# Six of seven projections by seven block products instead of eight, in a pooling and mLSTM trunk on one Trainium2 core

## The chip, the core and the metric

The kernel runs on one core of a Trainium2 chip. The core has five engines with queues of their own: TensorE (PE: matmuls; PEld: the loading of their stationary operand), VectorE (DVE), ScalarE (ACT), GpSimd (POOL) and SyncE (SP, which here issues every DMA). Matmuls read SBUF and write PSUM; everything else goes between SBUF and DRAM by DMA. The metric is the time of one execution on the device in microseconds (us), lower is better.

## The reference

One layer over 4096 rows (SEQ) of 1024 channels, in float32. Cut to what matters:

```
u = rmsnorm(x, norm_w)
pool_x, pool_z, m_x, m_z, m_o = split(u @ w_in, 5)       # 1024 columns each
# pooling branch: 4 groups of 256 channels, trailing windows 2, 4, 8, 16
d = window_mean(pool_x) - pool_x
y_pool = (d @ pool_w[group]) * pool_scale * silu(pool_z)
# mLSTM branch: 4 heads of 256
xc = silu(causal_conv4(m_x))
q, k, v = blockdiag(xc, xc, m_x);  i, f = gates(q, k, v)
h = mlstm_chunkwise(q, k, v, i, f)                      # chunks of 128 rows
hn = head_norm(sigmoid(m_o) * h) * mh_norm_w
y_mlstm = (hn + m_skip * xc) * silu(m_z)
out = rmsnorm(x + concat(y_pool, y_mlstm) @ w_out, final_norm_w)
```

There are seven products of a 4096 x 1024 matrix with a 1024 x 1024 one: the five parts of w_in and the two halves of w_out.

## The kernel before

Every float32 operand of a projection is split into a high part in a 32-bit matmul format and the rest (`split`, lines 88 to 90: ACT casts, DVE subtracts). `mm3` (lines 114 to 120) then makes a product as high by high, high by low and low by high, so one tile of 128 x 128 by 128 x 512 is three matmuls. One product of 512 rows with a 1024 x 1024 matrix is 4 x 2 x 8 such tiles, or 192 matmuls.

The work is in stages. **Pooling** (lines 139 to 302): eight blocks of 512 rows. `norm_u` (154 to 203) loads x transposed, makes the norm, keeps u in SBUF and stores it in DRAM (`u_d`); the block's u is split once and used for both the folded pooling projection (`fold`, 216 to 239: the group's map is multiplied into the weights beforehand) and its gate; products of the pooling go to `yp_d`. **mLSTM** (305 to 686): half blocks of 256 rows. `project` makes m_x and the convolution, `front` and `back` do one chunk of 128 rows each in steps, and the string `ORDER` (line 32) says in which order steps of front, back, next projection and convolution are issued. h goes to `h_d`, x_c to `xc_d`. In the last two chunks `gate_ahead` (401 to 416) computes the m_z gate of the last 256 rows in place of a next projection. **Gates** (690 to 774): per block of 512 rows u is loaded again, the m_z gate (`gate`) and m_o are projected, the head norm is made, `finish` transposes h and stores `ym_d`. **Output** (774 to 819): per 256 rows y_pool and y_mlstm are loaded and split, multiplied with w_out, x is added, the last norm made.

All DMAs stand in SP's queue, in the order that the scheduler of the language gives them; each engine runs its queue in order. Tiles come from pools with a fixed number of buffers, and an instruction waits until the buffer that it writes is free: weights come through two raw buffers (`wsp`), u tiles in pools of 19 or 18.

Of the kernel before, what the change touches and what calls it, by code (L numbers as in the profile page):

```python
# [12 lines left out]
ALU = mybir.AluOpType  # L13
# [6 lines left out]
NJ = D // P  # L20
T = 512
# [6 lines left out]
# gate tiles made ahead of the head norm  # L28
GA = 4
# [4 lines left out]
GW = P + 8  # L34


@with_exitstack
def tile_hybrid(
# [7 lines left out]
    pool_scale: bass.AP,  # L46
# [10 lines left out]
    NB = S // T  # L57
    DH = D // H

    const = ctx.enter_context(tc.tile_pool(name="const", bufs=1))  # L60
    w1p = ctx.enter_context(tc.tile_pool(name="w1p", bufs=16))
    stp = ctx.enter_context(tc.tile_pool(name="stp", bufs=4))
    wsp = ctx.enter_context(tc.tile_pool(name="wsp", bufs=2))
# [4 lines left out]
    col = const.tile([P, 64], F32, name="col")  # L68
# [5 lines left out]
    msk = col[:, 56:64]  # L74
    nhalf = const.tile([P, H], F32, name="nhalf")
    nc.vector.memset(nhalf, -0.5)

    u_d = [dram.tile([NJ, P, T], F32, name=f"u_d{b}") for b in range(NB)]
    yp_d = [dram.tile([NJ, P, T], F32, name=f"yp_d{b}") for b in range(NB)]
    ym_d = [dram.tile([NJ, P, T], F32, name=f"ym_d{b}") for b in range(NB)]  # L80
    xc_d = [dram.tile([NJ, P, T], F32, name=f"xc_d{b}") for b in range(NB)]
    sz_d = dram.tile([NJ, P, TB], F32, name="sz_d")
    h_d = [dram.tile([NCH, P, D], F32, name=f"h_d{b}") for b in range(NB)]

    def st():
        return stp.tile([P, D], F32, name="st")

    def split(raw, hi, lo):
        nc.scalar.copy(out=hi, in_=raw)  # L89
        nc.vector.tensor_tensor(out=lo, in0=raw, in1=hi.bitcast(F32), op=ALU.subtract)  # L90

    def load_w(src, n, pool, tag, stage=None):
        """src as [part, tile, column] in n tiles of 1024/n columns, split."""
        hi = pool.tile([P, D], F32R, name=tag)
        lo = pool.tile([P, D], F32R, name=tag)
        for h in range(2):
            raw = stage.tile([P, D // 2], F32, name="u") if stage else wsp.tile([P, D // 2], F32, name="ws")
            if n == 1:
                nc.sync.dma_start(out=raw, in_=src[:, 0, h * T:(h + 1) * T])
            else:  # L100
                nc.sync.dma_start(out=raw.rearrange("p (k c) -> p k c", k=n // 2),
                                  in_=src[:, h * n // 2:(h + 1) * n // 2, :])
            split(raw, hi[:, h * T:(h + 1) * T], lo[:, h * T:(h + 1) * T])
        return hi, lo

    def load_in_cols(c0, pool, tag, stage=None):
        """Columns c0..c0+127 of w_in by k tile: [k part, k tile, column]."""
        return load_w(w_in[:, c0:c0 + P].rearrange("(k p) c -> p k c", p=P), NJ, pool, tag, stage)

    def load_rows(w, r0, c0, n, pool, tag):  # L110
        """Rows r0.. in n tiles of 128, 1024/n columns from c0: [row part, tile, column]."""
        return load_w(w[r0:r0 + n * P, c0:c0 + D // n].rearrange("(k p) c -> p k c", p=P), n, pool, tag)

    def mm3(ps, pairs, start=True, stop=True):
        """ps = sum over pairs of (stationary hi, lo) with (moving hi, lo), without lo by lo."""
        n = len(pairs)
        for k, (a, b) in enumerate(pairs):
            nc.tensor.matmul(ps, lhsT=a[0], rhs=b[0], start=start and k == 0, stop=False)  # L118
            nc.tensor.matmul(ps, lhsT=a[0], rhs=b[1], start=False, stop=False)  # L119
            nc.tensor.matmul(ps, lhsT=a[1], rhs=b[0], start=False, stop=stop and k == n - 1)  # L120

    def kcol(pair, k):
        return tuple(t[:, k * P:(k + 1) * P] for t in pair)

    def proj_t(ps, wpair, u):
        mm3(ps, [(kcol(wpair, k), u[k]) for k in range(NJ)])

    def proj_part(ps, wpair, u, part):
        """Half of proj_t's k tiles."""
        mm3(ps, [(kcol(wpair, k), u[k]) for k in range(4 * part, 4 * part + 4)], part == 0, part == 1)  # L130

    def load_u(b, k0, k1, pool):
        u = []
        for k in range(k0, k1):
            lo = pool.tile([P, T], F32R, name="u")
            nc.sync.dma_start(out=lo.bitcast(F32), in_=u_d[b][k])
            u.append((pool.tile([P, T], F32R, name="u"), lo))
        return u

    # ---------------------------------------------------------------- pooling mixer  # L140
    with tc.tile_pool(name="a_u", bufs=19) as up, \
            tc.tile_pool(name="a_w2", bufs=16) as w2p, \
            tc.tile_pool(name="a_work", bufs=2) as wk, \
            tc.tile_pool(name="a_one", bufs=1) as one, \
            tc.tile_pool(name="a_tp", bufs=1, space=PSUM) as tpp, \
            tc.tile_pool(name="a_acc", bufs=6, space=PSUM) as accp:
        inv0 = one.tile([P, HALO], F32, name="inv0")
        nc.gpsimd.iota(inv0, pattern=[[1, HALO]], base=1, channel_multiplier=0,
# [726 lines left out]
```

## Time and profile before

| | us |
|---|---|
| median of 3 runs (3152.22 to 3162.3) | 3160.18 |
| the profiled execution: span from first to last instruction | 3157.9 |
| last wide matmul of the pooling stage starts | 751.7 |
| first wide matmul of the gates | 1731.5 |
| last wide matmul | 3150.5 |

A line of the page on an engine gives its busy time, the share of the span and its instructions. A line on a group gives source line, engine, operation, what is written and read, shape and count, then busy time and mean length of one in ns, then the idle time of the engine before it and what ended that. A window's line gives its length and then busy time and count of each engine, the granted TensorE clock (1.00 is full), the mean busy share of the 16 DMA engines and GB/s.

### The profile page before, as it was taken

The page shows a single profiled execution, that of the slowest core. Times are in us where ns is not written, and L with a number is a line of the kernel's source. Part 1 is how long each engine was busy: PE and PEld are TensorE (multiplying, and loading weights), DVE is VectorE, ACT ScalarE, POOL GpSimd, SP SyncE. Part 2 cuts the span into 40 slices and gives each one's busy share as a digit, 9 for nine tenths or more (in the row PEclk, how much of TensorE's full clock was granted, in tenths as well). Part 3 has the DMA queues.
Part 4 walks back from the last instruction along what each step waited for, and adds up shares of the span by engine and source line. Part 5 has one row for each costly group of instructions (what it writes and reads, how often), then busy time and mean ns, then how long its engine had stood idle before and what let it go on. Part 6 is the DMA issues. An engine that isn't in the chain of part 4 may idle for free.

```text
span 3157.9 us, 44492 instructions
## 1 busy us (share of the span) xinstructions
PE 3056.9 (97%) x16872; PEld 2659.8 (84%) x16872; DVE 1642.0 (52%) x3726; ACT 1162.2 (37%) x2464; POOL 573.8 (18%) x811
## 2 busy tenths in 40 slices
PE   7999999999899999999999999999999999999999
PEld 6888888888898998998998888888888788888887
DVE  5554444544788788888887443334436422222221
ACT  4221122223677677767776222222113311111111
POOL 1010010101354445444543000000000000000000
PEclk9999999999999999999999999999999999999999
DMA  6221111222111111112133223333215523222231
GB/s 210 87 77 70 61 67 60 77 97 75 61 55 58 51 54 62 50 51 64 51 91 112 76 93 107 107 107 107 68 59 173 184 100 107 94 92 96 94 107 50
DMA packets 189607, 273.57 MB, mean 87 GB/s; under 512 B 17232, under 2 KB 111952, under 8 KB 189392
## 3 DMA queue, kind: packets, MB, share of 16 engines
q1 hardware_dynamic: 189392, 270.72, 25.5%
q8 instruction: 133, 2.18, 0.3%
q14 instruction: 82, 0.67, 0.1%
HBM read 168.96 MB, written 101.71 MB: 86 GB/s over the span
## 4 chain that ended last, share of the span: by engine, by line
PE 86%; DVE 6%; DMA 3%; ACT 3%; issue 1%; SPq 1%; POOL 0%; POOLq 0%; DVEq 0%; ACTq 0%
PE acc L118 24%; PE acc L119 24%; PE acc L120 24%; DVE xc L370 3%; PE mm L603 2%; PE mm L628 2%; PE map L482 2%; PE mm L599 1%; DMA sk<-xc_d 1%; PE map L472 1%; PE map L493 1%; DMA ws<-in_w_out_dram 1%; PE acc L236 1%; DVE c L629 1%; PE tp L726 0%
## 5 line engine op out<-in xcount | busy, mean ns | idle before, releaser
L118 PE MATMUL acc<-u,w 128*128 128x512 f32 (+1 forms) x2592 | 907.3, 351 | 3.8 <-ACT mx L617 1.7
L120 PE MATMUL acc<-u,w 128*128 128x512 f32 (+1 forms) x2592 | 897.5, 346 | 0.0
L119 PE MATMUL acc<-u,w 128*128 128x512 f32 (+1 forms) x2592 | 895.5, 346 | 0.0
L118 PE MATMUL acc<-w,u 128*128 128x512 f32 x1536 | 598.4, 390 | 3.8 <-ACT w L89 2.8
L119 PE MATMUL acc<-w,u 128*128 128x512 f32 x1536 | 598.1, 390 | 0.2 <-DVE w L90 0.2
L120 PE MATMUL acc<-w,u 128*128 128x512 f32 x1536 | 597.5, 390 | 0.0
L118 PEld LDWEIGHTS acc<-u,w 128*128 128x128 f32 x2592 | 495.2, 191 | 64.2 <-ACT u L89 4.1
L119 PEld LDWEIGHTS acc<-u,w 128*128 128x128 f32 x2592 | 495.7, 191 | 58.6 <-DVE u L90 1.1
L120 PEld LDWEIGHTS acc<-u,w 128*128 128x128 f32 x2592 | 495.5, 191 | 57.4
L118 PEld LDWEIGHTS acc<-w,u 128*128 128x128 f32 x1536 | 288.5, 188 | 65.5 <-ACT w L89 3.6
L120 PEld LDWEIGHTS acc<-w,u 128*128 128x128 f32 x1536 | 288.9, 188 | 60.4 <-DVE u L790 0.6
L119 PEld LDWEIGHTS acc<-w,u 128*128 128x128 f32 x1536 | 288.6, 188 | 60.6 <-DVE w L90 0.7
L370 DVE SCALAR_TENSOR_TENSOR xc<-mx,col,xc 128x256 f32<-128x256 f32 x384 | 220.6, 632 | 30.5 <-POOL mx L447 22.3
L804 DVE TENSOR_TENSOR st<-acc,st 128x512 f32<-128x512 f32 x64 | 44.3, 692 | 364.9 <-PE acc L120 364.9
L356 POOL TENSOR_TENSOR cs<-c,cs 128x516 fp32r<-128x516 f32 x124 | 176.4, 1423 | 232.0 <-ACT cs L355 208.2
L757 POOL TENSOR_TENSOR rs<-rs,nhalf 128x2 f32<-128x2 f32 x64 | 44.6, 697 | 660.6 <-DVE rs L756 660.6
L789 ACT CAST u<-u 128x512 fp32r<-128x512 f32 x128 | 77.6, 619 | 230.7 <-PE acc L119 187.2
L811 ACT ACTIVATE sk<-st 128x1024 bf16<-128x1024 f32 x31 | 32.8, 1058 | 311.4 <-DVE st L804 311.4
L815 POOL TENSOR_TENSOR rso<-ssq,nhalf 128x1 f32<-128x1 f32 x32 | 17.4, 543 | 701.9 <-DVE ssq L812 701.9
L749 DVE SCALAR_TENSOR_TENSOR st<-th,st 128x512 f32<-128x512 f32 x64 | 44.3, 692 | 184.8 <-ACT th L747 184.7
L747 ACT ACTIVATE th<-acc 128x512 f32<-128x512 f32 x64 | 38.3, 598 | 273.4 <-PE acc L120 272.9
L599 PE MATMUL mm<-va,st 128*128 128x258 f32 x384 | 82.1, 310 | 52.3 <-DVE st L90 39.8
(181 smaller groups left out, 4201.9 us busy)
## 6 DMA issues: line engine op xcount, KB each, us to landing
u<-u_d SPq DMA_DIRECT2D x128, 256.0 KB, 3.9
st<-in_x_t_dram SPq DMA_DIRECT2D x32, 512.0 KB, 3.5
u_d<-st SPq DMA_DIRECT2D x32, 512.0 KB, 4.2
yp_d<-sg SPq DMA_DIRECT2D x64, 256.0 KB, 2.0
xc_d<-xc SPq DMA_DIRECT2D x64, 256.0 KB, 2.4
st<-h_d SPq DMA_DIRECT2D x32, 512.0 KB, 5.2
sk<-xc_d SPq DMA_DIRECT2D x64, 256.0 KB, 3.8
ym_d<-sg SPq DMA_DIRECT2D x64, 256.0 KB, 3.1
```

The source lines that it names most:

```text
L118: nc.tensor.matmul(ps, lhsT=a[0], rhs=b[0], start=start and k == 0, stop=False)
L119: nc.tensor.matmul(ps, lhsT=a[0], rhs=b[1], start=False, stop=False)
L120: nc.tensor.matmul(ps, lhsT=a[1], rhs=b[0], start=False, stop=stop and k == n - 1)
L356: nc.gpsimd.tensor_tensor(out=t[:, 1], in0=cst[h], in1=t[:, 0].bitcast(F32), op=ALU.subtract)
L370: nc.vector.scalar_tensor_tensor(out=a[:, t], in0=m[:, t, i:i + TB], scalar=conv_w[:, jj * 4 + i:jj * 4 + i + 1], in1=a[:, t], op0=ALU.mul ...
L482: nc.tensor.matmul(ps[:, i, :], lhsT=bqk[:, q * 4 + i, :], rhs=xc[q * 4 + i][:, l0:l0 + P], start=True, stop=True)
L599: nc.tensor.matmul(nps, lhsT=wt[:, w, h, :], rhs=vh[v], start=i == 0, stop=first and i == 2)
L603: nc.tensor.matmul(nps, lhsT=qi[h][:, w, t, :], rhs=cs[:, v, t], start=False, stop=t == 1 and i == 2)
L628: nc.tensor.matmul(upd, lhsT=xw[h][:, w, t * P:(t + 1) * P], rhs=vh[v], start=i == 0, stop=i == 2)
L749: nc.vector.scalar_tensor_tensor(out=hv, in0=th, scalar=1.0, in1=hv, op0=ALU.add, op1=ALU.mult)
L757: nc.gpsimd.tensor_tensor(out=rs, in0=rs, in1=nhalf[:, 0:2], op=ALU.pow)
L789: nc.scalar.copy(out=hi, in_=raw)
```

## The change

The pooling projection and its gate, the output gate, the m_z gate and both output projections are now made in "passes", each one 1024-column product over four blocks of 1024 rows. Rows, inner dimension and columns of a block are halved, and the eight products of quarters become seven, by sums of quarters on either side and sums of results. The m_x projection of the mLSTM stretch keeps eight.

- Left operands are kept in DRAM as quarters ready to use (`us_d`, `yp_d`, `ym_d`: a11, s2, a12, s3, s1, a22, s4, a21), so the sums are made once by `put_sums` where u or y is made, on POOL (for the first block half on DVE).
- Right operands are summed as they are loaded (`load_right`: raw tiles through a pool of 8, sums on POOL, then the split). A pass keeps its seven in SBUF; the next pass's are loaded during the last of its four blocks.
- `drive` runs 14 steps per block (7 products, two halves of the inner dimension, 24 matmuls each). Left tiles are fetched from DRAM and split for every pass, up to three steps ahead.
- Results are combined in `Item.after` on DVE, partly by accumulating two products in one PSUM bank. What follows a result (pooling, gate, head norm, residual, last norm) hangs on `done` of an item.
- The order is: two pooling passes (each half of the pooling columns with half of the gate's), the first output pass (x + y_pool w_out into `r_d`), mLSTM, output gate (into `hn_d`), m_z gate (into `ym_d`), second output pass and last norm.
- `norm_next` makes the next block's u during the first pass and loads its x twice. The mLSTM's weights are loaded at the end of the first output pass; `gate_ahead` is gone, and in its place the first four of the output gate's right operands are loaded. `pool_scale` is applied by ACT after the gate's SiLU instead of in the fold.

```
+A_OF = ("a11", "s2", "a12", "s3", "s1", "a22", "s4", "a21")
+NP = 7
+B_OF = (((1, 0, 0),),
+        ((1, 1, 1), (-1, 0, 1), (1, 0, 0)),
+        ((1, 1, 0),),
+        ((1, 1, 1), (-1, 0, 1)),
+        ((1, 0, 1), (-1, 0, 0)),
+        ((1, 1, 0), (-1, 1, 1), (1, 0, 1), (-1, 0, 0)),
+        ((1, 1, 1),))
+AHEAD = 4
...
+    def load_right(hi, lo, k, terms, sources, tile):
+        acc = None
+        for sign, kh, ch in terms:
+            t = tile()
+            rows, c0 = sources[ch]
+            nc.sync.dma_start(out=t, in_=rows(k + 4 * kh)[:, c0:c0 + T])
+            if acc is not None:
+                nc.gpsimd.tensor_tensor(out=acc, in0=acc, in1=t, op=ALU.add if sign > 0 else ALU.subtract)
+            else:
+                acc = t
+        split(acc, hi[:, k], lo[:, k])
...
+        def fetch(t):
+            n, r, i, kh = steps[t]
+            hi = ring.tile([P, 2, T], F32R, name="sr")
+            lo = ring.tile([P, 2, T], F32R, name="sr")
+            raw = lo.bitcast(F32)
+            nc.sync.dma_start(out=raw, in_=passes[n].left[r][i][:, 2 * kh:2 * kh + 2, :])
+            split(raw, hi, lo)
+            got[t] = hi, lo
...
+            for v in range(t, min(t + AHEAD, len(steps))):
+                if v not in got:
+                    fetch(v)
...
+            chain = "abab" "cbc"[i]
...
+                mm3(ps, pairs, start=kh == 0 and i in (0, 1, 4), stop=kh == 1, skip=True)
+                if kh == 1:
+                    f = p.items[q].after(r, i, ps)
...
+            if r + 1 == NR:
+                nxt = passes[n + 1] if n + 1 < len(passes) else None
+                free = i - 1 if kh == 0 else (i if i == NP - 1 else -1)
+                if free >= 0 and nxt:
+                    load(nxt, free)
...
+        def after(self, r, i, ps):
+            v = self.view
+            if i == 0:
+                self.s1 = self.tile()
+                nc.scalar.copy(out=v(self.s1), in_=ps)
+            elif i == 1:
+                self.u2 = self.tile()
+                nc.vector.tensor_tensor(out=v(self.u2), in0=ps, in1=v(self.s1), op=ALU.add)
+            elif i == 2:
+                return self.done(r, 0, 0, self.first(ps))
+            elif i == 3:
+                self.u3 = self.tile()
+                nc.vector.tensor_tensor(out=v(self.u3), in0=ps, in1=v(self.s1), op=ALU.add)
+            else:
+                t, rh, ch = ((self.u3, 1, 1), (self.s1, 1, 0), (self.u2, 0, 1))[i - 4]
+                nc.vector.tensor_tensor(out=v(t), in0=ps, in1=v(t), op=ALU.add)
+                return self.done(r, rh, ch, t)
...
+    with tc.tile_pool(name="a_w2", bufs=6) as w2p, \
+            tc.tile_pool(name="a_ring", bufs=8) as ring, \
+            tc.tile_pool(name="a_ch", bufs=17) as chp, \
+            tc.tile_pool(name="a_x", bufs=8) as xp, \
...
+        def norm_next(r):
+            ss = one.tile([P, 2, T], F32, name="ss")
+            for h in range(2):
+                for k in range(NJ):
+                    t = x_tile()
+                    x_load(t, r, k, h)
...
+            for k in range(4):
+                q = {}
+                for kk in (k, k + 4):
+                    for h in range(2):
+                        t = x_tile()
+                        x_load(t, r, kk, h)
+                        scaled(t, kk, ss[:, h])
+                        name = f"a{h + 1}{kk // 4 + 1}"
+                        put_quarter(us_d[r], name, k, t, put_now)
+                        q[name] = t
+                put_sums(us_d[r], k, q["a11"], q["a12"], q["a21"], q["a22"], x_tile, nc.gpsimd, put_now)
...
+        drive([*p_mix, p_out1], ring, w2p, psp, x_tile, background, load_wm)
...
+        drive([p_o, p_z, p_out2], ring, w2p, psp, x_tile, background)
```

More of the change, by code (lines that the diff above doesn't have):

```diff
@@ L89, in split @@
+    wf_d = [dram.tile([P, D], F32, name=f"wf_d{k}") for k in range(NJ)]
+    def split(raw, hi, lo, eng=None):
         nc.scalar.copy(out=hi, in_=raw)
[L90 to L114, printed above, removed]
+        (eng or nc.vector).tensor_tensor(out=lo, in0=raw, in1=hi.bitcast(F32), op=ALU.subtract)
+    def mm3(ps, pairs, start=True, stop=True, skip=False):
@@ L116, in mm3 @@
         n = len(pairs)
         for k, (a, b) in enumerate(pairs):
[L118 to L143, printed above, removed]
+            nc.tensor.matmul(ps, lhsT=a[0], rhs=b[0], start=start and k == 0, stop=False, skip_group_check=skip)
@@ new lines, in start, with loads, squares, slot @@
+        def start():
+            ss = one.tile([P, 2, T], F32, name="ss")
+            xs = {}
+            def loads(h):
+                for k in range(NJ):
+                    xs[k, h] = chp.tile([P, HALO + T], F32, name="ch")[:, 0:T]
+                    x_load(xs[k, h], 0, k, h)
+            def squares(h):
+                for k in range(NJ):
+                    if k == 0:
+                        nc.scalar.activation(out=ss[:, h], in_=xs[k, h], func=AF.Square)
+                    else:
+                        sq = x_tile()
+                        nc.scalar.activation(out=sq, in_=xs[k, h], func=AF.Square)
+                        nc.vector.tensor_tensor(out=ss[:, h], in0=ss[:, h], in1=sq, op=ALU.add)
+            free = []
+            def slot():
+                if not free:
+                    t = w2p.tile([P, 4, T], F32, name="w2")
+                    free.extend(t[:, i] for i in range(4))
+                return free.pop(0)
+            loads(0)
+            folds = [fold(g, slot) for g in range(2)]
+            next(folds[0])
+            loads(1)
+            next(folds[1])
+            squares(0)
+            root(ss[:, 0])
+            for _ in folds[0]:
+                pass
+            for _ in folds[1]:
+                pass
+            for k in range(NJ):
+                scaled(xs[k, 0], k, ss[:, 0])
+                put_quarter(us_d[0], ("a11", "a12")[k // 4], k % 4, xs[k, 0], put_now)
+            squares(1)
+            root(ss[:, 1])
+            for k in range(4):
+                for kk in (k, k + 4):
+                    scaled(xs[kk, 1], kk, ss[:, 1])
+                    put_quarter(us_d[0], ("a21", "a22")[kk // 4], k, xs[kk, 1], put_now)
+                a21 = x_tile()
+                nc.scalar.copy(out=a21, in_=xs[k, 1])
+                put_sums(us_d[0], k, xs[k, 0], xs[k + 4, 0], a21, xs[k + 4, 1], x_tile,
+                         (nc.vector, nc.gpsimd)[k % 2], put_now)
@@ new lines, in tile_hybrid, with background @@
+        p_mix = [Pass(us_d, [(wf_rows, n * T), (in_rows, D + n * T)], [Mix(n, c) for c in range(4)], False)
+                 for n in range(2)]
+        p_out1 = Pass(yp_d, halves(out_rows(0), 0), [Sum(q) for q in range(4)], True)
+        start()
+        norms = [norm_next(r) for r in range(1, NR)]
+        folds = [fold(g, x_tile) for g in range(2, H)]
+        def background(n, r, m):
+            if n == 0 and r + 1 < NR:
+                for _ in range({0: 1, 1: 1, 2: 1, 3: 1, 6: 1, 7: 1, 8: 1, 9: 1, 10: 2}.get(m, 0)):
+                    next(norms[r])
+            if n == 0 and r in (1, 2) and m in (11, 12, 13):
+                next(folds[r - 1], None)
```

693 lines of the change are left out of this document (414 added, 279 removed).

## The prediction

> **What bounds the kernel now.** I read the page's shares and chain first, then the windows by stage, then the groups of lines with shapes kept apart, then the DMA queue and its issues.
>
> ```profile
> span 3157.9 us, 44492 instructions
> PE 3056.9 (97%) x16872; PEld 2659.8 (84%) x16872; DVE 1642.0 (52%) x3726; ACT 1162.2 (37%) x2464; POOL 573.8 (18%) x811
> PE 86%; DVE 6%; DMA 3%; ACT 3%; issue 1%; SPq 1%; POOL 0%; POOLq 0%; DVEq 0%; ACTq 0%
> core 0: us, PE busy (x) PEld busy (x) DVE busy (x) ACT busy (x) POOL busy (x), PEclk, DMA share, GB/s
> 0.00:26.00 26.00, 10.94 (x37) 8.79 (x37) 14.87 (x27) 12.54 (x20) 3.61 (x10) 1.00 0.74 224
> 26.00:752.00 726.00, 725.04 (x3196) 600.06 (x3196) 360.53 (x561) 176.54 (x301) 63.66 (x137) 1.00 0.24 83
> 752.00:765.00 13.00, 11.25 (x66) 10.84 (x66) 4.47 (x14) 5.89 (x28) 0.98 (x9) 0.68 0.75 228
> 765.00:1731.00 966.00, 898.90 (x7176) 873.65 (x7176) 769.83 (x2122) 673.60 (x1623) 443.56 (x560) 0.96 0.19 61
> 1731.00:2457.00 726.00, 720.31 (x3370) 597.06 (x3370) 312.30 (x737) 174.53 (x291) 44.63 (x64) 1.00 0.31 104
> 2457.00:3158.00 701.00, 690.52 (x3031) 569.40 (x3031) 179.98 (x269) 119.15 (x203) 17.39 (x32) 0.99 0.29 100
> ```
>
> The chain is PE for 86%, and the windows show where: in the pooling stage (26 to 752) and in the last two (1731 to 3158) PE is busy all but 1 to 11 us of 700, while DVE stands at 26 to 50%, POOL at 2 to 9% and the DMA engines at 24 to 31%. Only the mLSTM stretch is mixed (PE 93%, DVE 80%, POOL 46%). A busy PE need not be PE at its peak, so the price of a matmul is read from their starts: PE's timeline at 2700 us, first and last of 55 rows, and the groups by shape.
>
> ```profile
> 2699.61 0.39 PE L120 MATMUL acc<-w,u 128*128 128x512 f32 x1
> ...
> 2711.85 0.39 PE L120 MATMUL acc<-w,u 128*128 128x512 f32 x1
> L118 PE MATMUL acc<-w,u 128*128 128x512 f32 x1536 | 598.4, 390 | 3.8 <-ACT w L89 2.8 <-ACT u L789 1.0
> L118 PE MATMUL acc<-u,w 128*128 128x512 f32 x1472 | 574.7, 392 | 3.4 <-ACT mx L617 1.7 <-ACT u L89 1.5
> L118 PE MATMUL acc<-u,w 128*128 128x256 f32 x1120 | 332.5, 298 | 0.4 <-ACT xc L453 0.4
> 1709.09 0.28 PE L120 MATMUL acc<-u,w 128*128 128x256 f32 x1
> ...
> 1711.25 0.28 PE L120 MATMUL acc<-u,w 128*128 128x256 f32 x1
> ```
>
> 12.24 us over 54 steps is **0.2267 us** for one 128x512 matmul, though its own record lasts 0.39; the 256-column form (2.16 us over 18 steps at 1709 us) takes 0.12. Lines 118 to 120 run alike, so 3 x (1536 + 1472) = 9024 of them take 2046 us. The time is bought with matmuls.
>
> **What the change removes.** Six projections over four blocks of 1024 rows are 6 x 4 x 384 matmuls by eight block products, 6 x 4 x 336 = 8064 by seven. 8064 x 0.2267 = 1828 us; so 218 us less of the wide form, and also gone are 384 of the 256-column form at 0.12 (the gate of the last rows, half of it run ahead in the mLSTM stretch): 264 us of PE in all. One block of one pass is now 336 x 0.2267 = 76.2 us of PE, a pass 305, a step of 24 matmuls 5.4.
>
> **What it adds: sums and splits.** Nearest rows:
>
> ```profile
> L90 DVE TENSOR_TENSOR w<-ws,w 128x512 fp32r<-128x512 f32 x80 | 54.4, 688 | 48.0 <-ACT w L89 47.6
> L89 ACT CAST w<-ws 128x512 fp32r<-128x512 f32 x80 | 48.9, 620 | 78.7 <-DMA ws<-in_w_in_dram 37.8 <-DMA ws<-in_w_out_dram 30.4 <-PE acc L119 8.7
> L434 POOL TENSOR_TENSOR u<-u 128x512 fp32r<-128x512 f32 x64 | 85.3, 1335 | 105.3 <-ACT u L433 105.3
> L817 DVE SCALAR_TENSOR_TENSOR st<-st,rso,fw 128x1024 f32<-128x1024 f32 x31 | 39.8, 1285 | 22.3 <-POOL rso L815 22.3
> L753 DVE BATCH_NORM_STATS2 stats<-st 128x6 f32<-128x256 f32 x128 | 48.2, 418 | 2.1
> L754 DVE BATCH_NORM_AGGREGATE mv<-stats 128x2 f32<-128x6 f32 x128 | 19.2, 173 | 0.0
> ```
>
> DVE in one block of the output-gate pass, the fullest plain one: 14 splits of 1024 columns at 1.285 (18), 20 adds out of PSUM at 0.69 (14), 16 products with h (11), 32 statistics at 0.418 and 0.173 (19), small ones (5): 67 us beside 76 of PE. POOL in the first pass: 16 adds of sums, 14 of squares, 8 products at 1.335 and small copies, about 60. Both lie beside PE, and I cost them at nothing. In the block in which the next pass's weights are loaded, 28 splits (DVE 19) and 28 adds (POOL 37) come on top: DVE 86, POOL 76 to 80. That cover is gone there, and the excess of up to 10 us is taken to lie under the transfers, below. Each left tile is fetched three steps (16 us) ahead, and landing, cast and subtract take 3.9 + 1.1 + 1.3, so a single fetch is hidden.
>
> **What it adds: transfers.** This is the term that decides. Everything now goes through DRAM: seven left quarters per block and pass, the sums, the residual, the normalised h.
>
> ```profile
> q1 hardware_dynamic: 189392, 270.72, 25.5%
> u<-u_d SPq DMA_DIRECT2D x128, 256.0 KB, 3.9
> st<-in_x_t_dram SPq DMA_DIRECT2D x32, 512.0 KB, 3.5
> u_d<-st SPq DMA_DIRECT2D x32, 512.0 KB, 4.2
> ws<-in_w_in_dram SPq DMA_DIRECT2D x48, 256.0 KB, 3.1
> ws<-in_w_out_dram SPq DMA_DIRECT2D x32, 256.0 KB, 3.3
> w<-in_wx_t_dram SPq DMA_DIRECT2D x8, 512.0 KB, 7.9
> ```
>
> I count in tiles of 256 KB (0.262 MB). Per block: left operand 28 in each pass. First pooling pass: 32 loads of x (twice 16), 32 stores of u and its sums, 8 of the product, 100 in all for the first three blocks and 36 for the last; 9 for a folded group in two blocks. Second: 8 products, 8 reads, 16 sums, 60. First output pass 60; output gate 28 + 16 h + 16 stores = 60; gate path 28 + 16 + 16 + 28 = 88; last pass 60. The weights of a pass are 14 terms x 4 = 56 tiles, all but the mLSTM's 16 loaded in the last block of the pass before (the output gate's half in the mLSTM stretch, half in its first block). The whole is some 2290 tiles, 600 MB against 271.
>
> At what rate? The best that 20 us of this trace held, a start, and the rest:
>
> ```profile
> 2000.00:2020.00 20.00, 19.52 (x95) 15.68 (x94) 10.67 (x17) 8.72 (x15) 0.00 (x0) 1.00 0.88 310
> 20.00:50.00 30.00, 27.55 (x122) 22.54 (x121) 24.86 (x41) 17.99 (x31) 4.06 (x5) 1.00 0.86 282
> ```
>
> 310 GB/s at a share of 0.88 would be 352 at a share of 1; the start held 282 over 30 us and 224 over 26. I take **310**, 0.846 us a tile, the nearest row that is a burst of these same tile loads, and keep 352 and 224 as ends (2991 and, by 1.17 us a tile and 103 us in each other block of the gate path, 3432). The 512-byte rows of the h tiles cost nothing more: the weight columns (512-byte rows) land in 3.1 us, the output weights (2 KB rows) in 3.3. Where tiles x 0.846 is under PE's time, the transfer is hidden; where it is over, it sets the time:
> - first pass with the launch: start 16 + 32 + 18, weights 56, blocks 100 + 109 + 109, last block 36 + 56: 532 tiles, 450 us, against some 365 of PE work (305, the folds and the launch);
> - last block of the second pooling pass: 60 + 56 = 116 tiles, 98 us against 76;
> - last block of the output gate: the same, 98;
> - last block of the gate path: 88 + 56 = 144 tiles, 122 us against 85 (its 64 transposes are a quarter of 36 us);
> - all other blocks: at most 88 tiles, 74 us, hidden under 76 to 85.
>
> ```profile
> L726 PE MATMUL tp<-ident,st 128*128 128x128 f32 x256 | 36.2, 274 | 4.3 <-DVE sk L727 4.2
> L599 PE MATMUL mm<-va,st 128*128 128x258 f32 x384 | 82.1, 310 | 52.3 <-DVE st L90 39.8 <-DVE c L629 11.1 <-ACT st L89 1.3
> ```
>
> By the Trainium skill ("DMA: Bandwidth & Descriptors", "Where 436 GB/s comes from") the HBM side limits a core to about 358 GB/s. No stretch here reaches that (310 is the most quoted); by that figure the 908 tiles of the four places would take 665 us and the sum below would be an estimated 2980.
>
> **The mLSTM stretch** (752 to 1731, 979 us) keeps its work. It loses 192 narrow matmuls: between nothing (DVE is the busier engine at its end) and 192 x 0.12 = 23 us; its waits on DVE and POOL stay (the L599 row: 52 us idle, most of it for DVE), so I take 10. At its start buffers come free only with the pooling passes, as before; 5 us more for constants that lay outside those buffers. At its end the next left tile can be fetched only when its buffers are released: 3.9 + 1.1 + 1.3 and the queue, 8 us, where the kernel before had u in place.
>
> **The sum**, against the span of 3157.9: pooling side 450 + (305 + 22) + 305 = 1082; mLSTM 979 - 10 + 5 = 974; last side 8 + (305 + 22) + (305 + 36 + 37) + 305 + 7 (the tail now) = 1025. That is **3081**, and with the 2.3 us that lie between span and median (3160.2), **3083 us**. Of the 264 us on PE, transfers, launch and stage borders take back some 187.
>
> **The rivals.**
> 1. *The transfers run at full share* (352): 908 x 0.745 = 676 us instead of 768, so 2991. For it: a share of 0.88 was met at a time when demand came in bursts. Against: that the queue is never full. With no transfer in the way at all the floor is 365 + 76 + 76 + 85 for those four places, 2917.
> 2. *The eight staging buffers set the time; slower than before.* x tiles, weight terms, sums and h tiles share eight buffers of 256 KB in either stage. A tile holds one from its issue through landing, adds on POOL (1.335 each) and often a store; SP's queue is in order, so a load that waits for a buffer holds back the left fetches behind it, and PE waits for these. The blocks ask for 112 + 63 + 63 + 56 such lives in the first pass (weights 56, x 32, sums 12, norm 12, fold 7) and 76, 72 and 100 in the three other places: 542, or 68 us for each us of a life, and some 60 of launch. The point: 845 us for these places, total 3160, at a life of 11.6 us. By the rows a weight term lives 3.3 + 1.3 + 0.6 + 0.7 = 6 us on a quiet queue and 10 to 11 at the launch's 7.9 to landing; an x tile of the norm 3.5 + 3 x 0.7 + 4 x 1.3 + 4.2 = 15. At 14 us the total is 3323. Against it: the two kinds mix to about 10, and then the rate decides.
> 3. *The gain is just given back*: at the rate of the launch, 282, the 908 tiles take 844 us, so 3159.
> 4. *It does not save matmuls*: the count of the wide form would be 9024 still; the code gives 336 per block, I give it no chance of its own.
>
> The clock gate adds little to these. In the border at 752 the granted clock fell to 0.68. By the Trainium skill ("TensorE: Matmul & The Clock Gate", Part 1) an idle window of 3.4 us halves it; where transfers decide PE has slack for that, so I add nothing.
>
> **How the numbers follow.** Forecast (3030 to 3150) 0.44; rival 1 and anything below 3030: 0.26; rival 3: 0.08; rival 2: 0.22. Measured differences under 0.3% are no change: faster 0.70, same 0.08, slower 0.22. The range: 2955 (rate 352 and half of the borders) to 3200 (270 GB/s, or a life of 12.2 us) leaves some 0.2 out.
>
> **What would show it.** Wide matmuls on PE: 8064, 0.227 us apart, in the plain blocks without gaps. First pass ends near 450 us with DMA share above 0.85 throughout and PE near 70%; PE waits there for casts that wait for DMA. The last blocks of the second, output-gate and gate-path passes are 20 to 40 us longer than their others, with POOL above 70%. mLSTM within 15 us of 979. Wrong if: the DMA share in the first pass stays under 0.7 while PE idles (rival 2), the plain blocks take over 80 us (DVE or fetch distance), or the first pass takes under 400.

## The result, and the profile after

The change makes the kernel slower: 3447.39 us (median of 4 runs, 3445.09 to 3451.58) against 3159.57 (4 runs), a ratio of 1.092 (95% interval 1.0903 to 1.0934). The forecast, 3083 us and faster, missed in size and sign. First the page's head of the changed kernel: span, busy time by engine, the DMA queue, the chain by engine.

```profile
span 3447.9 us, 45998 instructions
PE 2894.1 (84%) x15528; PEld 2480.1 (72%) x15528; DVE 2255.8 (65%) x4262; ACT 1528.0 (44%) x2915; POOL 1357.0 (39%) x1329
q1 hardware_dynamic: 328128, 599.53, 52.6%
PE 38%; DVE 15%; DMA 10%; POOL 9%; ACT 7%; issue 5%; SPq 1%; POOLq 0%; DVEq 0%; ACTq 0%
```

PE is busy 163 us less than before (3056.9), but idle for 554 us instead of 101: 453 more, less 163, is the 290 by which the span grew. The chain was PE for 86%; now PE has 38%, and DVE, POOL and ACT together have 31%. The bytes are the 600 MB that were forecast. The engine windows below are single blocks: the first three of the first pooling pass, the last of the second, the first two of the first output pass, and the last of the gate path (columns as before).

```profile
core 0: us, PE busy (x) PEld busy (x) DVE busy (x) ACT busy (x) POOL busy (x), PEclk, DMA share, GB/s
72.50:216.30 143.80, 95.41 (x345) 72.55 (x345) 101.21 (x118) 53.66 (x84) 92.55 (x76) 0.81 0.69 229
216.30:378.00 161.70, 93.51 (x376) 75.14 (x377) 72.96 (x89) 46.44 (x69) 79.17 (x65) 0.77 0.66 220
378.00:510.50 132.50, 88.34 (x378) 71.90 (x377) 67.22 (x83) 43.50 (x65) 66.09 (x56) 0.85 0.66 217
873.70:982.40 108.70, 85.22 (x337) 67.78 (x336) 75.04 (x83) 39.11 (x58) 68.47 (x53) 0.87 0.71 230
982.40:1119.20 136.80, 87.18 (x337) 68.54 (x336) 69.55 (x76) 25.82 (x31) 49.74 (x36) 0.80 0.73 242
1119.20:1195.40 76.20, 76.20 (x338) 63.09 (x337) 40.85 (x54) 14.72 (x14) 0.00 (x0) 1.00 0.65 218
2967.60:3103.50 135.90, 93.42 (x402) 73.99 (x401) 65.10 (x74) 49.82 (x75) 85.01 (x60) 0.86 0.83 267
```

The plain block of the output pass takes the forecast 76.2 us with PE never idle and POOL at rest. In the heavy blocks, those that take well over that, nothing is full: the DMA engines' share is 0.66 to 0.83, not above 0.85 as forecast. In most of them DVE and POOL are both much at work: 101 + 93 us in a block of 144, 65 + 85 in one of 136 (less so in the first block of the output pass, 70 + 50 of 137). Some plain blocks are slow, too: the first three of the second pooling pass take 92 to 96 us at a DMA share of 0.46 to 0.54. By place, each from one block's first wide matmul to the next, in us:

| place | forecast | changed | sums on DVE | and loads one group ahead |
|---|---|---|---|---|
| launch and first pass | 450 | 590 | 534 | 504 |
| second pooling pass | 327 | 392 | 352 | 367 |
| first output pass | 305 | 365 | 347 | 344 |
| mLSTM and its end | 982 | 995 | 996 | 992 |
| output gate | 327 | 322 | 320 | 323 |
| gate path | 378 | 439 | 395 | 389 |
| last pass and tail | 312 | 344 | 333 | 334 |

(The two right columns are experiments below.) Next, groups of the changed kernel by line with shapes apart, in the page's form:

```profile
L112 DVE TENSOR_TENSOR w<-x,w 128x512 fp32r<-128x512 f32 x168 | 155.6, 950 | 92.4 <-ACT w L111 91.0
L112 DVE TENSOR_TENSOR sr<-sr 128x1024 fp32r<-128x1024 f32 x336 | 456.5, 1359 | 596.4 <-ACT sr L111 584.8 <-DMA x<-in_w_in_dram 10.1 <-PE ps L120 1.0
L291 DVE TENSOR_TENSOR ch<-ps,ch 128x512 f32<-128x512 f32 x288 | 193.9, 682 | 70.6 <-PE ps L120 69.6
L130 POOL TENSOR_TENSOR x<-x 128x512 f32<-128x512 f32 x156 | 243.2, 1566 | 182.1 <-DMA x<-in_w_in_dram 115.1 <-DMA x<-in_w_out_dram 40.9 <-DMA sr<-us_d 9.9
```

The split of a right operand was priced at 688 ns and takes 950, POOL's additions at 1335 and take 1566. The instructions of L291, which read one operand from PSUM, kept their 682. The timelines of DVE and then POOL in the gate path's last block show what the slow ones stand beside (start us, us):

```profile
3050.52 1.31 DVE L112 TENSOR_TENSOR w<-x,w 128x512 fp32r<-128x512 f32 x1 [2.38 <-ACT w L111]
3051.75 0.68 DVE L291 TENSOR_TENSOR ch<-ps,ch 128x512 f32<-128x512 f32 x1
3052.35 1.18 DVE L112 TENSOR_TENSOR w<-x,w 128x512 fp32r<-128x512 f32 x1
3053.46 0.68 DVE L291 TENSOR_TENSOR ch<-ps,ch 128x512 f32<-128x512 f32 x1
3054.06 1.18 DVE L112 TENSOR_TENSOR w<-x,w 128x512 fp32r<-128x512 f32 x1
3055.16 0.68 DVE L291 TENSOR_TENSOR ch<-ps,ch 128x512 f32<-128x512 f32 x1
3055.76 0.68 DVE L112 TENSOR_TENSOR w<-x,w 128x512 fp32r<-128x512 f32 x1
```

```profile
3049.99 4.70 POOL L130 TENSOR_TENSOR x<-x 128x512 f32<-128x512 f32 x3 [0.15 <-issue]
```

POOL's three additions end at 3054.7. The splits that begin before that take 1.18 to 1.31 us, the one after it 0.68; the additions out of PSUM take 0.68 all along. Over the whole trace, the 85 such splits that overlap POOL's work for less than a tenth of their time take 684 ns on average, the other 83 take 1222. By the Trainium skill ("SBUF — State Buffer", "Who interferes with whom") a VectorE instruction with two SBUF inputs contends with a GpSimd instruction that reads SBUF, and one with at most one SBUF input doesn't, outside the modes that use both ports. The trace agrees on both (684 to 1222 ns, and 682 whatever POOL does); the prediction had not drawn on it.

The list of waits names who was late (engine, line, releaser; us in all, times, longest):

```profile
DVE sr L112 <- ACT sr L111: 584.8, 172, 18.3
ACT sr L111 <- DMA sr<-us_d: 505.7, 135, 29.2
ACT sr L111 <- DMA sr<-yp_d: 214.6, 46, 17.2
ACT w L111 <- POOL x L130: 181.6, 61, 9.4
ACT sr L111 <- DMA sr<-ym_d: 168.0, 42, 16.1
PE ps L398 <- DMA x<-in_wx_t_dram: 82.6, 2, 41.4
```

They offer four suspects: left tiles that land late (888 us of ACT), for want of rate or because of the order of the queues; sums on POOL (182); and two waits of PE for the loads of a fold (83). Idle time of an engine doesn't say which of these sets the end, so each was taken away. In the expectations, the rate theory is that the DMA engines can move no more; the order or queue theory, that work stands in an in-order queue behind other work that waits; the buffer or staging theory, that the eight staging buffers and the chain of load, sum and store through them set the time.

### The profile page after: what moved, and what is told of

It is laid out like the page before. It is cut to its first block, busy times and chain, and to the rows that moved or that the text cites. A ratio compares the mean times of both kernels' runs of the same rounds, so it can differ in the third digit from the quotient of the medians.

```text
span 3447.9 us, 45998 instructions
## 1 busy us (share of the span) xinstructions
PE 2894.1 (84%) x15528; PEld 2480.1 (72%) x15528; DVE 2255.8 (65%) x4262; ACT 1528.0 (44%) x2915; POOL 1357.0 (39%) x1329
## 4 chain that ended last, share of the span: by engine, by line
PE 38%; DVE 15%; DMA 10%; POOL 9%; ACT 7%; issue 5%; SPq 1%; POOLq 0%; DVEq 0%; ACTq 0%
PE ps L118 8%; PE ps L120 8%; PE ps L119 8%; DVE xc L696 4%; POOL x L130 2%; DMA sr<-us_d 2%; PE acc L118 2%; PE acc L120 2%; PE acc L119 2%; DVE w L112 2%; DVE sr L112 2%; PE mm L909 1%; DMA x<-in_w_out_dram 1%; DVE wk L515 1%; DMA sr<-ym_d 1%
## 5 line engine op out<-in xcount | busy, mean ns | idle before, releaser
L112 DVE TENSOR_TENSOR sr<-sr 128x1024 fp32r<-128x1024 f32 x336 | 456.5, 1359 | 596.4 <-ACT sr L111 584.8
L111 ACT CAST sr<-sr 128x1024 fp32r<-128x1024 f32 x336 | 352.5, 1049 | 947.1 <-DMA sr<-us_d 505.7
L118 PE MATMUL ps<-sr,w 128*128 128x512 f32 x1344 | 546.8, 411 | 155.8 <-ACT sr L111 115.9
L118 PE MATMUL ps<-w,sr 128*128 128x512 f32 x1344 | 533.0, 397 | 72.2 <-ACT sr L111 50.6
L119 PE MATMUL ps<-sr,w 128*128 128x512 f32 x1344 | 545.6, 406 | 36.2 <-DVE sr L112 36.1
L120 PE MATMUL ps<-sr,w 128*128 128x512 f32 x1344 | 542.7, 404 | 0.0
L120 PE MATMUL ps<-w,sr 128*128 128x512 f32 x1344 | 530.4, 396 | 13.2 <-DVE sr L112 13.1
L119 PE MATMUL ps<-w,sr 128*128 128x512 f32 x1344 | 530.0, 394 | 0.0
L118 PEld LDWEIGHTS ps<-sr,w 128*128 128x128 f32 x1344 | 265.9, 199 | 221.4 <-ACT sr L111 123.7
L118 PEld LDWEIGHTS ps<-w,sr 128*128 128x128 f32 x1344 | 257.1, 191 | 130.7 <-ACT sr L111 64.5
L119 PEld LDWEIGHTS ps<-sr,w 128*128 128x128 f32 x1344 | 264.9, 197 | 103.7 <-DVE sr L112 48.2
L130 POOL TENSOR_TENSOR x<-x 128x512 f32<-128x512 f32 x156 | 243.2, 1566 | 182.1 <-DMA x<-in_w_in_dram 115.1
L120 PEld LDWEIGHTS ps<-w,sr 128*128 128x128 f32 x1344 | 256.1, 191 | 75.5 <-DVE sr L112 21.9
L120 PEld LDWEIGHTS ps<-sr,w 128*128 128x128 f32 x1344 | 263.9, 196 | 56.5 <-DVE w L112 0.4
L119 PEld LDWEIGHTS ps<-w,sr 128*128 128x128 f32 x1344 | 256.8, 191 | 53.5
L118 PE MATMUL acc<-u,w 128*128 128x256 f32 x992 | 291.5, 294 | 0.4 <-ACT xc L759 0.4
L120 PE MATMUL acc<-u,w 128*128 128x256 f32 x992 | 283.0, 285 | 0.0
L119 PE MATMUL acc<-u,w 128*128 128x256 f32 x992 | 281.0, 283 | 0.0
L291 DVE TENSOR_TENSOR ch<-ps,ch 128x512 f32<-128x512 f32 x288 | 193.9, 682 | 70.6 <-PE ps L120 69.6
L112 DVE TENSOR_TENSOR w<-x,w 128x512 fp32r<-128x512 f32 x168 | 155.6, 950 | 92.4 <-ACT w L111 91.0
```

The costliest lines, as they stand in the source:

```text
L112: (eng or nc.vector).tensor_tensor(out=lo, in0=raw, in1=hi.bitcast(F32), op=ALU.subtract)
L130: nc.gpsimd.tensor_tensor(out=acc, in0=acc, in1=t, op=ALU.add if sign > 0 else ALU.subtract)
L291: nc.vector.tensor_tensor(out=v(t), in0=ps, in1=v(t), op=ALU.add)
```

## The experiments

Each is one execution, beside one of the kernel before (3158.5 to 3162.6 us). Differences under 10 us are not read. Where not said otherwise, the edit is made on the changed kernel (3447).

**The order of the queues.** The left fetches on ACT's queue instead of SP's; the folds of groups 2 and 3 made ahead of the first pass (their generators are started in `start` and run there instead of in `background`); both.

```
-            nc.sync.dma_start(out=raw, in_=passes[n].left[r][i][:, 2 * kh:2 * kh + 2, :])
+            nc.scalar.dma_start(out=raw, in_=passes[n].left[r][i][:, 2 * kh:2 * kh + 2, :])
...
-            folds = [fold(g, slot) for g in range(2)]
+            folds = [fold(g, slot) for g in range(H)]
```

> Only the queue of the left fetches changes: ScalarE issues them instead of SP, so that no load or store that waits in SP's queue stands in front of them. Order theory (the one DMA queue holds back left fetches behind transfers that wait for sums on POOL or for a staging buffer): the waits at the third product of the second pass's blocks (3 x 13 to 15 us), at the start of the first output pass (44), of the gate path (22) and of the last pass (13), and part of those at the first pass's block borders go: 3447 falls to 3230 to 3330. Rate theory (this mix of transfers gets no more than about 240 GB/s): the same bytes at the same rate, within 30 us of 3447. Buffer theory (the eight staging buffers): within 30 us of 3447, since they are as busy as before.

> The folds of groups 2 and 3 are made in the launch, like those of groups 0 and 1, and not in the first pass's second and third block, where PE waited 41.4 and 41.2 us for their loads. Order theory: PE's queue is in order and these two waits are lost time, so 65 to 85 us go from the two blocks and the launch grows by some 5 to 15: 3365 to 3390. Rate theory: the bytes are the same and PE's wait was only where the shortage of transfers showed; the wait moves to the next fetches, 3430 to 3450. Buffer theory: 14 of some 126 buffer lives leave these two blocks, so they fall by 10%, 25 to 30 us: 3420.

> Both edits together. Order theory: they act on different waits and add up, 3150 to 3260. Rate theory: within 30 us of 3447. Buffer theory: about 3420.

Measured were 3455.76, 3440.35 and 3444.05. The second block of the first pass did shorten without its fold (161.8 to 124.6 us), but launch and the last block gave most of that back. Removing 83 us of waiting moved the end by 7: something behind it was as late. Left fetches on ACT's queue shorten one block much, the first of the first output pass (136.8 to 105.3), and lengthen others by as much (the output gate from 322 to 356). So this order of the queues gains nothing in all; a queue that holds left fetches alone was not tried.

**PE.** Only the high by high matmul in the six passes.

```
+            if skip:
+                continue
             nc.tensor.matmul(ps, lhsT=a[0], rhs=b[1], start=False, stop=False, skip_group_check=skip)
```

> The changed kernel with only the high by high matmul of each block product (the two others are left out in the six passes; the mLSTM stretch is whole). A step is 1.8 us of PE instead of 5.4, all transfers and sums stay. What is left of a block's time is what the transfers, sums and splits take by themselves. Rate theory at 240 GB/s: 100 tiles take 109 us, 60 tiles 66, the first pass stays at 560 to 590, the whole at 3150 to 3300. Order theory: the first pass stays above 450 but the plain blocks (60 tiles, 76 us now) fall to 50 to 55, with the DMA share over 0.8 there, the whole at 2700 to 2950. Buffer theory: blocks with few staged tiles fall to a third, those with weights stay.

Measured: 3177.36. Two thirds of 8064 matmuls, 1219 us of PE, are gone and the time falls by 270. The first three blocks stay at 140.0, 153.9 and 126.9 us. These blocks do not wait for PE. The value fitted the rate theory, but also any other by which PE isn't the limit.

**Sums against transfers.** Four runs. First, all sums on DVE:

```
-                nc.gpsimd.tensor_tensor(out=acc, in0=acc, in1=t, op=ALU.add if sign > 0 else ALU.subtract)
+                nc.vector.tensor_tensor(out=acc, in0=acc, in1=t, op=ALU.add if sign > 0 else ALU.subtract)
...
-                put_sums(us_d[r], k, q["a11"], q["a12"], q["a21"], q["a22"], x_tile, nc.gpsimd, put_now)
+                put_sums(us_d[r], k, q["a11"], q["a12"], q["a21"], q["a22"], x_tile, nc.vector, put_now)
...
```

> All the sums of staging (of right operands, of the norm, of left operands) go from POOL to DVE, where one costs 0.7 to 0.95 us against 1.57 us on POOL; transfers are the same 600 MB. Staging theory (the eight staging buffers are held through a serial chain load, sum, store, and POOL's share of it is on the path): the heavy blocks lose what POOL's part of their chains shortens by, some 28 us in each block that loads the next pass's right operands (5 of them) and some 14 us in each of the first three blocks: 3260 to 3370. Rate theory (mixed reads and writes move 220 to 250 GB/s here, whatever is done with them): 3420 to 3475.

Measured: 3278.08. The page's engine line and the groups:

```profile
PE 2869.7 (88%) x15528; PEld 2468.4 (75%) x15528; DVE 2380.6 (73%) x4648; ACT 1530.6 (47%) x2915; POOL 812.1 (25%) x943
L112 DVE TENSOR_TENSOR w<-x,w 128x512 fp32r<-128x512 f32 x168 | 113.3, 699 | 18.0 <-ACT w L111 17.2
L130 DVE TENSOR_TENSOR x<-x 128x512 f32<-128x512 f32 x156 | 108.0, 704 | 30.0 <-DMA x<-in_w_in_dram 18.3 <-DMA x<-in_w_out_dram 9.1 <-DMA x<-wf_d 2.0
```

DVE has 386 instructions more, some 270 us at the 704 ns of such a sum, yet its busy time rose by only 125 (2255.8 to 2380.6). So about 145 us of DVE's time in the changed kernel was the price of POOL's work beside it. The table above shows the gain where the sums stood: first pass, second pass, gate path.

In the second run the parts of a right operand are loaded and not added; in the third the norm's loads and stores stay and its arithmetic goes.

```
-            if acc is not None:
-                nc.gpsimd.tensor_tensor(out=acc, in0=acc, in1=t, op=ALU.add if sign > 0 else ALU.subtract)
-            else:
+            if acc is None:
                 acc = t
```

> Every part of a right operand is loaded as before, but only the first is used: the 28 additions on POOL of each pass are left out, so the output is not the reference's; the bytes stay. Staging theory: the last block of every pass loses most of its excess (79.8, 108.7, 85.9 and 136.0 us in the run with the change; the last would fall under 105) and the first block of the next pass too: 3300 to 3390. Rate theory: within 25 us of 3447, block by block.

```
-                        nc.scalar.activation(out=t, in_=t, func=AF.Square)
-                        nc.gpsimd.tensor_tensor(out=ss[:, h], in0=ss[:, h], in1=t, op=ALU.add)
...
-                root(ss[:, h])
...
-                        scaled(t, kk, ss[:, h])
...
-                put_sums(us_d[r], k, q["a11"], q["a12"], q["a21"], q["a22"], x_tile, nc.gpsimd, put_now)
+                for name, t in zip(("s2", "s3", "s1", "s4"), q.values()):
+                    put_quarter(us_d[r], name, k, t, put_now)
```

> In the first pass, the norm of the blocks to come keeps its 32 loads and 32 stores a block, but squares, root, scaling and sums between them are left out (what is stored is the loaded data, so the output is not the reference's). Rate theory: the first three blocks stay at 143, 162 and 132 us within 10 us each, time 3420 to 3450. Staging theory: they fall towards what their transfers take at the best rate seen, some 105 us each: 3300 to 3350.

Measured were 3348.53 and 3344.36, both times as the staging theory had them. Windows of the first three blocks without the norm's arithmetic:

```profile
73.00:204.70 131.70, 90.71 (x337) 69.25 (x337) 74.39 (x94) 44.88 (x65) 61.21 (x54) 0.84 0.88 290
204.70:301.10 96.40, 87.78 (x369) 71.89 (x369) 47.55 (x57) 32.75 (x43) 19.19 (x25) 0.93 0.94 314
301.10:393.00 91.90, 85.12 (x371) 70.32 (x369) 43.35 (x54) 29.60 (x41) 18.24 (x22) 0.96 0.91 299
```

In the second and third block, the work that took 161.7 and 132.5 us at 220 and 217 GB/s now takes 96.4 and 91.9 at 314 and 299. The rate was there; the arithmetic between load and store kept it from being used. The rate theory falls for these two. The first block misses the 105 us expected of each: it moves 290 GB/s for 131.7 us, or 146 tiles of 256 KB, since part of the pass's own weights are loaded in it. At 310 GB/s these would take an estimated 123 us, so there the bytes themselves leave little to gain.

The fourth has twelve staging buffers, paid for with two tiles of the ring (the buffers of the left tiles); its control has the small ring alone.

```
-AHEAD = 4
+AHEAD = 3
...
-            tc.tile_pool(name="a_ring", bufs=8) as ring, \
+            tc.tile_pool(name="a_ring", bufs=6) as ring, \
-            tc.tile_pool(name="a_x", bufs=8) as xp, \
+            tc.tile_pool(name="a_x", bufs=12) as xp, \
```

> Twelve staging buffers instead of eight in both projection stages, paid for with two ring tiles fewer (left operands fetched 3 half products ahead instead of 4). Staging theory: a third to a half of the 354 us by which the heavy blocks exceed the prediction goes: 3270 to 3340, and the share of the DMA engines in the first three blocks rises above 0.75. Rate theory: 3430 to 3480, since the same bytes move at the same rate and the ring has less in hand.

> The change with a ring of six left tiles and fetches three steps ahead, but eight staging buffers: the run with twelve buffers and the same ring took 3525.89. Staging buffers: at least 40 us slower than that run, 3570 to 3650. If the number of buffers does not matter: 3510 to 3540, and the ring alone costs the 78 us.

Measured: 3525.89 with twelve and 3526.15 with eight. With this ring the number of staging buffers changes nothing, and the smaller ring with its one step less of fetch distance costs 78 us. Twelve buffers with a ring of eight were not tried.

**On top of sums on DVE**: the folds first; these with left fetches on ACT; and POOL kept busy beside DVE on a tile nobody reads.

> The run with sums on DVE, and besides only the folds of groups 2 and 3 ahead of the first pass. If those two PE waits (28.5 and 27.3 us) are on the path now: 3225 to 3245, with some 9 us more before the first pass. If the chain through the staging buffers covers them, as it did with the sums on POOL (3440 against 3447): 3265 to 3290.

> The run with sums on DVE (3278.08), and besides the folds of groups 2 and 3 ahead of the first pass and the left fetches on ACT's queue. With POOL off the path the order of SP's queue may now be what is late next. Order: the two PE waits for fold loads (28.5 and 27.3 us) go and the left fetches no longer stand behind loads that wait for a staging buffer: 3170 to 3225. Staging (the chain load, sum, store through eight buffers still sets the heavy blocks, whatever the queue): 3250 to 3290.

```
+    def beside():
+        for z in spare:
+            for _ in range(4):
+                nc.gpsimd.tensor_tensor(out=z, in0=z, in1=z, op=ALU.mult)
```

> The run with sums on DVE, and beside every such sum of the pooling stage four products of 128 columns on POOL, on a tile that nobody reads: POOL is about as busy as in the run with the change, but no sum depends on it. If what cost was that the sums stood on POOL (1.57 us in the chain against 0.70): 3275 to 3300. If what cost was that POOL at work slows DVE's two-input instructions beside it (950 ns against 699 for the 512-column split of the right operand): the pooling stage, 1233 us until the mLSTM stretch with sums on DVE and some 1350 with the change, gives back over half of the difference, 3340 to 3400.

Measured were 3259.16 (folds first gain 19 us, between the two expectations), 3315.28 (left fetches on ACT cost 56 on top of that, outside both expectations) and 3620.64. The last misses its question: nothing paced the 1016 products, so POOL ran them in one go, and the norm's root and the pooling's copies, which POOL also makes, queued behind. The first two blocks took 300 and 257 us, the later ones were those of sums on DVE. It is a third way for POOL to hold up the kernel, not a measure of the second.

**Waits for landings in ACT's queue.** `fetch` issues a load and at once its split, so ACT stands waiting with other work queued behind it. The split is moved one step later, first alone, then with sums on DVE and folds first, then with the loads of the norm and of short right operands one group ahead of their arithmetic, too.

```
-            split(raw, hi, lo)
-            got[t] = hi, lo
+            raws[t] = raw, hi, lo
...
+            for v in range(t, min(t + AHEAD - 1, len(steps))):
+                if v not in got:
+                    cut(v)
```

> The change, with the split of each left tile one step (of 24 matmuls) after its fetch instead of right behind it; nothing else moved. Queue theory (ACT waits for each landing with the rest of its work behind it): ACT's waits for left tiles, 888 us in the run with the change, fall under 400, the first three blocks and the last ones of the passes shorten by 10 to 30 us each, 3250 to 3380. If ACT's waits cover nothing (the chain through POOL's sums and DVE is the limit): the waits fall but the time stays within 30 us of 3447, or grows, since the split has one step less in hand.

> The run with sums on DVE and folds first (3259.16), with the split one step after the fetch. Queue theory: 3120 to 3200. Otherwise: 3235 to 3290.

> The run before it, and the loads of the norm's groups and of right operands of one or two terms issued one group ahead of their arithmetic, through the same eight buffers. Queue theory: landings no longer stand in ACT's and DVE's queues, a further 30 to 90 us less than the run with the late split alone, 3060 to 3160, first three blocks under 100 us each. Otherwise: within 25 us of that run.

Measured were 3462.26, 3258.24 and 3255.06. In the first, ACT's waits for left tiles fell under 400 us as expected (from us_d 505.7 to 203.4, from yp_d 214.6 to 24.0, from ym_d 168.0 to 94.6), and the time did not fall. In their place ACT waits 482 us for PE, 5.3 at most at a time: there it is ahead of PE. Removing most of the largest waits in the list gained nothing, and the queue theory falls.

**What then?** The last three start from the 3255 us of the run with loads ahead: less DVE work with the same bytes, fewer bytes with the same work, and every other sum back on POOL.

```
-            split(raw, hi, lo)
+            nc.scalar.copy(out=hi, in_=raw)
+            nc.vector.tensor_tensor(out=lo[:, :, 0:32], in0=raw[:, :, 0:32], in1=hi.bitcast(F32)[:, :, 0:32], op=ALU.subtract)
```

> The run before (3255.06), with the subtraction that makes the low part of a left tile done on 32 of its 512 columns only (the rest of the low part keeps the raw data, so the output is not the reference's): 14 subtractions of 1.22 us a block, some 15 us, go from DVE; the bytes stay. If elementwise work on DVE sets the heavy blocks: each of the ten that take over 80 us shortens by 8 to 15 us, 3100 to 3180. If the transfers set them: 3235 to 3260.

```
+                    if n % 2:
+                        got[k, h] = got[keys[n - 1]]
+                        continue
                     got[k, h] = x_tile()
                     x_load(got[k, h], r, k, h)
```

> The run with loads one group ahead (3255.06), with half of the norm's loads and 20 of the 56 right-operand loads of a pass left out and the neighbour's tile used in their place (so the output is not the reference's): 168 tiles, 44 MB, fewer; the arithmetic stays in number and place. If the transfers set the heavy blocks: the first three shorten by some 14 us each and those that load right operands by some 15, 3120 to 3190. If elementwise work does: 3225 to 3260.

```
-                    nc.vector.tensor_tensor(out=acc, in0=acc, in1=t, op=ALU.add if sign > 0 else ALU.subtract)
+                    (nc.vector, nc.gpsimd)[k % 2].tensor_tensor(out=acc, in0=acc, in1=t, op=ALU.add if sign > 0 else ALU.subtract)
...
```

> The run with loads one group ahead (3255.06), with every other sum (k odd) on POOL. If DVE's own work is the limit and POOL is free help: 3190 to 3235. If POOL's additions beside it slow DVE (684 ns alone, 1242 beside POOL for the 512-column split in the run with the change) and lengthen the chain: 3275 to 3350.

Measured were 3192.62, 3242.51 and 3357.07. With less on DVE 62 us go, 39 of them in the second pooling pass (plain blocks 87 to 90 before, 78 to 80 now, and the whole pass at the forecast 327), but only 7 in the first pass and 4 in the gate path. DVE's work holds up the one pass, though DVE was busy only 69 us of 89 in its blocks, and the others little; the run misses its expected range. With 44 MB less the second and third block of the first pass go from 108.5 and 103.4 to:

```profile
204.00:310.50 106.50, 82.65 (x344) 65.89 (x344) 82.24 (x112) 40.83 (x60) 23.96 (x26) 0.88 0.61 202
310.50:418.80 108.30, 82.92 (x344) 66.11 (x344) 83.31 (x113) 40.83 (x61) 24.34 (x28) 0.88 0.62 204
```

The DMA share falls from 0.77 and 0.75 to 0.61 and 0.62, and the length stays. This run is not a clean one, though: where two uses share a tile, the second waits for the square, the sum or the store of the first, and in these two blocks ACT and DVE wait 25 us for such steps (1 us before). So it does not exclude that the bytes count there. And half of the sums back on POOL costs 102 us, a little more than the range expected for POOL slowing DVE and lengthening the chain. The engine lines of the run with loads ahead and then of this one:

```profile
PE 2871.4 (88%) x15528; PEld 2467.4 (76%) x15528; DVE 2395.1 (74%) x4648; ACT 1528.4 (47%) x2915; POOL 824.8 (25%) x943
```

```profile
PE 2900.8 (86%) x15528; PEld 2484.3 (74%) x15528; DVE 2356.7 (70%) x4476; ACT 1526.4 (45%) x2915; POOL 1069.4 (32%) x1115
```

POOL took 172 instructions and 245 us. They were worth 120 us on DVE at 700 ns, but DVE's busy time fell by only 38: the help took back two thirds of itself, and each sum stood twice as long in its chain.

## Why the prediction was wrong, point by point

- *Matmuls.* Right: 8064, and 76.2 us for a block in which nothing else holds PE up. PE's busy time fell by 163 us rather than 264, though; see the clock.
- *Bytes and their rate.* The 600 MB were right. 310 GB/s was not too high either, since 299 to 314 were moved in the first pass once the norm's arithmetic was out, and the last block of the gate path, forecast at 122 us, takes 119 at 300 GB/s in the run with loads one group ahead. The error was that transfers "decide" alone: with the sums on POOL these blocks moved 217 to 267. The bytes also lie in other blocks than the tally had them: the first block of the first output pass moves 242 GB/s for 136.8 us, or 126 tiles, where 60 were counted, because weights, y_pool's sums and loads of x of its neighbours fall into it. At 310 GB/s that is an estimated 107 us for 76, about half of the 60 us by which this pass missed.
- *Sums and splits: the step that failed.* "Both lie beside PE, and I cost them at nothing", and "the excess of up to 10 us is taken to lie under the transfers". That step added up each engine alone, with durations from a kernel in which POOL stood at 2 to 9% outside the mLSTM stretch. Here splits of right operands take 950 ns for 688, additions on POOL 1566 for 1335, and a block of the norm is a chain: load, scale, four sums one after the other, store. Moving the sums from POOL to DVE gives 169 us back; leaving out the norm's arithmetic or the right operands' sums alone gives 103 and 99. How the 169 divide between longer chains and slower DVE instructions stays open; the run meant for it did not answer that. Even where no weights are loaded the step fails: the plain blocks of the second pooling pass, 67 us of DVE at most beside 76 of PE by the prediction, take 92 to 96, over the 80 that it had set down as a sign of being wrong.
- *Rival 2.* Its sign was right (3323 at a life of 14 us, 3447 measured), and so was the failure sign set down for it: a DMA share under 0.7 in the first pass while PE idles. Of its mechanism the runs bear out that POOL's additions hold the blocks up (as links of the chain, or by slowing DVE, which the rival did not have). They do not bear out the eight buffers (twelve do no better with the smaller ring), nor a gain from taking the left fetches out of SP's queue. With 0.22 it had too little: its own rows gave a weight term 6 us on a quiet queue and 10 to 11 at the launch, and an x tile 15, around a point of decision at 11.6, and "about 10" leaned to the low end.
- *Rivals 1 and 3* hung on the rate alone and fall with it; *rival 4* did not come.
- *The clock gate*, to which I added nothing. In the first block PE was busy 95.4 us for 345 matmuls, 78.2 at full pace, at a granted clock of 0.81. PE's timeline after a wait of 21.7 us:

```profile
245.10 1.22 PE L118 MATMUL ps<-sr,w 128*128 128x512 f32 x2 [21.74 <-ACT sr L111]
...
248.66 0.63 PE L119 MATMUL ps<-sr,w 128*128 128x512 f32 x1
249.08 0.63 PE L120 MATMUL ps<-sr,w 128*128 128x512 f32 x1
...
250.38 0.39 PE L118 MATMUL ps<-sr,w 128*128 128x512 f32 x1
250.61 0.39 PE L119 MATMUL ps<-sr,w 128*128 128x512 f32 x1
```

  For some 5 us the matmuls start 0.43 us apart, then 0.23. This agrees with the rule of the Trainium skill that the prediction cited ("TensorE: Matmul & The Clock Gate", Part 1). By the trace's clock records PE was busy for 260 us at half the clock, against 80 in the kernel before. The 180 us more are an estimated 90 us of lost work, most of the 101 by which the saving on PE fell short (163 for 264); what it does to the end was not tried.
- *mLSTM and output gate.* 995 for 982 and 322 for 327 are right within 1 to 2%. For the output gate that is partly luck: its last block takes 85.9 us where 98 were forecast, its first two 78.7 and 81.5 for 76, and the errors cancel.
- *The folds.* Two waits of 41 us for their loads were not foreseen. Removing them gains 7 us in the changed kernel, too little to read, and 19 with the sums on DVE.

What stays open: the best version with the whole computation, 3255 us, is still 95 slower than the kernel before, and 172 above the forecast. Less work on DVE was worth 62 of it. What sets the first pass (504 for 450) is not shown: less on DVE gave 7 us there, and the run with fewer bytes put waits in their place; with the norm's arithmetic left out, and the other sums still on POOL, it took 474. No version with the whole computation beats the kernel before.

## What to carry to other kernels

Work that trades matmuls for sums has to be priced on the engines that make the sums, as a chain and with the slowdown that they cause each other. A duration from a trace in which POOL is idle is a lower bound for a DVE instruction with two SBUF inputs once POOL works beside it. When a block is late and nothing in it is full, take one resource at a time away: here the largest waits, 888 us in all, were worth nothing, and one of 182 led to 169.

## What the runs showed of the hardware

- A 128x512 subtraction on DVE with both inputs in SBUF takes 1.8 times as long beside POOL's work (684 to 1222 ns); an addition with one input in PSUM takes no longer (682). POOL's additions of that shape go from about 1.3 us to 1.57 on average. Spreading this kernel's sums over both engines was slower than leaving them all on DVE (3357 against 3255).
- One core moved 314 GB/s of mixed loads and stores at a share of 0.94 for 96 us, so 220 at a share of 0.66 was not the most that the DMA engines can do.
